# Hybrid decoder block: the order of the first projections, the engines of their weight splits, and transposes whose results nobody reads

## The chip, the cores and the metric

The kernel runs on one core of a Trainium2 chip. The metric is device time in microseconds (us): the median of three runs of the unprofiled kernel. Beside it there is one profiled execution, from which all rows below come. Lower is better.

## The reference

One layer over 1024 tokens, to which 16 learned meta tokens are prepended (1040 in all), with 1024 features:

```
u    = rms_norm(h, norm_mix)                      # h: 1040 x 1024
proj = u @ w_in                                   # attention A, attention B, xc, yc, gates
xc   = causal_depthwise_conv(xc)                  # width 4
o_c  = rg_lru(xc) * gelu(yc)                      # recurrence over tokens, 512 channels
o_a  = sliding_window_attention(.., rel_bias)     # 8 heads, relative bias table
o_f  = forgetting_attention(..)                   # 8 heads
h    = h + (sum_g sigmoid(gate_g) * (o_g @ w_branch_g)) @ w_out
h    = h + swiglu(rms_norm(h, norm_ffn))
out  = rms_norm(h, norm_final)[16:]
```

Only the start of this concerns the change: the first norm, the projections of xc and yc for the first two of four groups of 128 channels, and the relative bias table (32 buckets x 8 heads, gathered by a matrix product with a one-hot table of 383 distances).

## The kernel before

All matrix products are made in three terms: each operand is split into a high part (rounded to TensorE's short fp32 form, a copy on ScalarE) and a low part (the difference, on VectorE, or on GpSimd where `lo_on_pool` is given), and `mm3` (L143) adds high x high, high x low and low x high, for 8 slices of 128 features: 24 matmuls for each group of 128 channels and each chunk of tokens.

The tokens come in nine tiles: tile 0 holds the 16 meta tokens, tiles 1 to 8 hold 128 tokens each. `load_x` fetches a tile (512 KB, four buffers), `normed` squares and sums it on ScalarE (L297), takes the root there (L298), the reciprocal on VectorE (L299), and multiplies by that and the gain row `gbc` on VectorE in two halves (L301). `to_feature_major` (L198) then makes eight 128x128 transposes on TensorE (L204), four to a PSUM bank, and splits each bank into `uh` and `ul` (L118 on ScalarE, L119 on VectorE).

`proj_chunk` projects one chunk of tokens for one group of channels. The chunks are written out by hand:

```
FULL = ((0, 0, 272, 0), (0, 272, 256, 272), (1, 0, 512, 528))   # block, offset, tokens, position
REAL = ((0, NM, 512, 0), (1, 0, 512, 512))
```

`FULL` serves xc (meta tokens too), `REAL` serves yc. `FULL[0]` needs tiles 0, 1 and 2; `FULL[1]` needs tiles 3 and 4; `REAL[0]` needs tiles 1 to 4; `FULL[2]` and `REAL[1]` need tiles 5 to 8.

Before the change the order in the program is: tiles 0, 1, 2; the bias table's product; the two weight groups `wx` of xc (high part L137 on ScalarE, low part L138 on GpSimd); tiles 3 and 4; `FULL[0]` and `FULL[1]` of xc for both groups; the weights `wy` of yc (low part on GpSimd too); tiles 5 and 6; `REAL[0]` of yc for group 0; tiles 7 and 8; the bias table's spread over 128 partitions by two transfers (`bb`, then `bss`); `REAL[0]` for group 1; then `FULL[2]` and `REAL[1]` for both groups. All of this lives in a pool `r0`, whose memory the next stage (the recurrence, with the third and fourth group's projections as its main stream) takes over tile by tile as it comes free.

All transfers are issued from SyncE's queue. A scheduler orders each engine's instructions by their place in the program and by its own estimate of when their inputs are ready, so that an engine's order is not always that of the text. `keep_in_program_order` pins an instruction to its place; `issue_after(x)` queues the instructions of a block that run on x's engine behind x.

Of the kernel before, what the change touches and what calls it, by code (L numbers as in the profile page):

```python
# [9 lines left out]
F32 = mybir.dt.float32  # L10
F32R = mybir.dt.float32r
AF = mybir.ActivationFunctionType
ALU = mybir.AluOpType
# [3 lines left out]
P = 128  # L17
D = 1024
KT = D // P
NM = 16  # L20
# [14 lines left out]
QA, KA, QF, KF, XC, YC, GT = 0, 4, 5, 9, 13, 17, 21  # L35
# [11 lines left out]
def f32(ap):  # L47
    return ap.bitcast(F32)
# [3 lines left out]
def hybrid_block(ctx, tc, h_in, w_in, w_v0, w_v1, w_bd, par, rows, gains, relt, onehot,  # L52
                 maskrow, cmask, w_br, w_out, w_fi, w_fo, out):
    nc = tc.nc
    act, dve, pool, pe = nc.scalar, nc.vector, nc.gpsimd, nc.tensor

    def dma(dst, src):
        nc.sync.dma_start(f32(dst) if dst.dtype == F32R else dst, f32(src) if src.dtype == F32R else src)
# [8 lines left out]
    wp = ctx.enter_context(tc.tile_pool(name="wstream", bufs=2, side="left"))  # L67
# [11 lines left out]
    def nm(s):  # L79
        uid[0] += 1  # L80
        return f"{s}_{uid[0]}"

    def bank(tag, bufs, label):
        return pp.tile([P, 512], F32, tag=tag, bufs=bufs, name=nm(tag + label))
# [4 lines left out]
    o_bank = lambda label="": bank("ob", 1, label)  # L89
# [6 lines left out]
    ident = cp.tile([P, P], F32, name="ident")  # L96
    make_identity(nc, ident)
    cmt = cp.tile([P, P], F32, name="cmt")
    part = cp.tile([P, 40], F32, name="part")
    rowt = cp.tile([P, 16], F32, name="rowt")  # L100
    nsink = cp.tile([P, 8], F32, name="nsink")
# [13 lines left out]
    def split(hi, lo, src, scale=None, pin=False):  # L115

        if scale is None:
            act.activation(hi, src, AF.Copy)  # L118
            i = dve.tensor_tensor(lo, src, f32(hi), ALU.subtract)  # L119
            if pin:  # L120
                tc.keep_in_program_order(i)
        else:
            act.activation(hi, src, AF.Copy, scale=scale)
            dve.scalar_tensor_tensor(lo, src, scale, f32(hi), ALU.mult, ALU.subtract)

    def load_w(src, n, pl=None, tag="w", bufs=None, lo_on_pool=False):
        pl = pl or wp
        kw = {} if bufs is None else dict(bufs=bufs)
        if n == D:
            raw = wp.tile([P, n], F32, tag="wr", name=nm("wr"))  # L130
        else:
            raw = pl.tile([P, n], F32, tag=tag + "r", name=nm(tag + "r"), **kw)
        dma(raw, src)
        hi = pl.tile([P, n], F32R, tag=tag + "h", name=nm(tag + "h"), **kw)
        lo = pl.tile([P, n], F32R, tag=tag + "l", name=nm(tag + "l"), **kw)
        if lo_on_pool:
            act.activation(hi, raw, AF.Copy)  # L137
            pool.tensor_tensor(lo, raw, f32(hi), ALU.subtract)  # L138
        else:
            split(hi, lo, raw)  # L140
        return hi, lo
# [12 lines left out]
    def run(gen):  # L154
        for _ in gen:
            pass
# [41 lines left out]
    def to_feature_major(xg, n, uh, ul, off):  # L198

        for half in range(2):  # L200
            pt = tr_bank()
            for i in range(4):
                k = 4 * half + i
                pe.transpose(pt[:, i * P:i * P + n], xg[:n, k * P:(k + 1) * P], ident[:n, :n])  # L204
            src = pt.rearrange("p (i q) -> p i q", i=4)[:, :, :n]
            ks = slice(4 * half, 4 * half + 4)
            split(uh[:, ks, off:off + n], ul[:, ks, off:off + n], src)

    def u_tile(c, a):
        if c:  # L210
# [4 lines left out]
    uh = [u_tile(c, "h") for c in range(2)]  # L215
    ul = [u_tile(c, "l") for c in range(2)]
    FULL = ((0, 0, 272, 0), (0, 272, 256, 272), (1, 0, 512, 528))
    REAL = ((0, NM, 512, 0), (1, 0, 512, 512))

    def proj_chunk(j, w, chunk, sink):  # L220
        c, off, n, t0 = chunk
        ps = mm_bank(f"_w{j}")
        yield from mm3(ps[:, :n], [(w[0][:, k * P:(k + 1) * P], w[1][:, k * P:(k + 1) * P],
                                    uh[c][:, k, off:off + n], ul[c][:, k, off:off + n]) for k in range(KT)])
        sink(ps, n, t0)
# [36 lines left out]
    def x_sinks(pl, m):  # L262
        xr = pl.tile([P, 3 + T], F32, tag="xr", bufs=4, name=nm("xr"))
        y = pl.tile([P, S], F32, tag="y", bufs=4, name=nm("y"))
        pool.memset(xr[:, 0:3], 0.0)
        lru_in[m] = (xr, y)

        def xsink(ps, n, t0):
            act.activation(xr[:, 3 + t0:3 + t0 + n], ps[:, :n], AF.Copy)

        def ysink(ps, n, t0):
            act.activation(y[:, t0:t0 + n], ps[:, :n], AF.Copy)
        return xsink, ysink

    ra = ctx1.enter_context(tc.tile_pool(name="ra", bufs=1, side="right", reuse_waits="tile"))
    pad(ra, 128)
    with tc.tile_pool(name="r0", bufs=1, side="right", reuse_waits="tile") as r0:
        gbc = r0.tile([P, D], F32, name="gbc")

        def rows_of(t):  # L280
            return (NM, 0) if t == 0 else (P, NM + (t - 1) * P)

        def load_x(t):
            n, t0 = rows_of(t)
            xt = r0.tile([P, D], F32, tag="xt", bufs=4, name=nm("xt"))
            dma(xt[:n], h_in[t0:t0 + n])
            return xt

        def norm_in(t, xt):
            to_feature_major(*normed(t, xt))  # L290

        def normed(t, xt):
            n, t0 = rows_of(t)
            c, off = (0, t0) if t0 < W0 else (1, t0 - W0)
            xg = r0.tile([P, D], F32, tag="xg", bufs=3, name=nm("xg"))
            q = cp.tile([P, 1], F32, tag="sq", bufs=4, name=nm("sq"))
            act.activation(xg[:n], xt[:n], AF.Square, accum_out=q[:n])  # L297
            act.activation(q[:n], q[:n], AF.Sqrt, bias=epst[:n], scale=1.0 / D)  # L298
            dve.reciprocal(q[:n], q[:n])  # L299
            for x, y, z in zip(*(halves(v[:n]) for v in (xg, xt, gbc))):  # L300
                dve.scalar_tensor_tensor(x, y, q[:n], z, ALU.mult, ALU.mult)  # L301
            return xg, n, uh[c], ul[c], off

        xts = [load_x(t) for t in range(2)]
        dma(gbc, gains[0:1].partition_broadcast(P))
        xts.append(load_x(2))
        n0, n1 = normed(0, xts[0]), normed(1, xts[1])
        to_feature_major(*n1)
        n2 = normed(2, xts[2])
        to_feature_major(*n0)  # L310
        to_feature_major(*n2)

        dma(cmt, cmask)
        rt = r0.tile([32, 8], F32, name="rt")
        oh = r0.tile([32, 383], F32, name="oh")
        mr = r0.tile([8, 383], F32, name="mr")
        dma(rt, relt)
        dma(oh, onehot)
        dma(mr, maskrow.partition_broadcast(8))
        pb = sc_bank()  # L320
        pe.matmul(pb[:8, :383], rt, oh, start=True, stop=True)
        dve.tensor_tensor(mr, pb[:8, :383], mr, ALU.add)
        sinks = [x_sinks(ra, m) for m in range(2)]
        wx = [load_w(w_in[XC + m], D, r0, f"x{m}", lo_on_pool=True) for m in range(2)]
        xs34 = [load_x(t) for t in (3, 4)]
        n34 = [normed(t, xs34[t - 3]) for t in (3, 4)]
        for m in range(2):
            run(proj_chunk(XC + m, wx[m], FULL[0], sinks[m][0]))
            if m == 0:
                to_feature_major(*n34[0])  # L330
                to_feature_major(*n34[1])
        for m in range(2):
            run(proj_chunk(XC + m, wx[m], FULL[1], sinks[m][0]))
        xs56 = [load_x(t) for t in (5, 6)]
        wy = [load_w(w_in[YC + m], D, lo_on_pool=True) for m in range(2)]
        for t in range(5, 7):
            norm_in(t, xs56[t - 5])
        run(proj_chunk(YC, wy[0], REAL[0], sinks[0][1]))
        for t in range(7, 9):
            norm_in(t, load_x(t))  # L340
        dma(part, par)
        dma(rowt, rows.partition_broadcast(P))
        dve.tensor_scalar(nsink, rowt[:, 0:8], -1.0, None, ALU.mult)
        dma(bts, mr)
        pad(r0, 32)
        bb = r0.tile([P, 8, 383], F32, name="bb")
        dma(bb, bts.partition_broadcast(P))
        dma(bss, bb)
        run(proj_chunk(YC + 1, wy[1], REAL[0], sinks[1][1]))
        for m in range(2):  # L350
            run(proj_chunk(XC + m, wx[m], FULL[2], sinks[m][0]))
        for m in range(2):
            run(proj_chunk(YC + m, wy[m], REAL[1], sinks[m][1]))
# [477 lines left out]
    with tc.tile_pool(name="r4", bufs=1, side="right", reuse_waits="tile") as r4:  # L831
        woh = r4.tile([P, KT, D], F32R, name="woh")
        wol = r4.tile([P, KT, D], F32R, name="wol")
        with tc.tile_pool(name="r4a", bufs=1, side="right", reuse_waits="tile") as r4a:
# [8 lines left out]
            for m in range(8):  # L843
                f, raw = ahead
# [13 lines left out]
        with tc.tile_pool(name="r4b", bufs=1, side="right", reuse_waits="tile") as r4b:  # L858
            for c in range(2):
                u2[c] = [pair_tile(mp if c else bp) for k in range(KT // 2)]  # L860
                for tt in range(4 * c, 4 * c + 4):
# [4 lines left out]
                    for half in range(2):  # L866
                        n = slice(512 * half, 512 * half + 512)
# [8 lines left out]
                    for half in range(2):  # L876
                        pt = tr_bank()
                        for i in range(4):
                            k = 4 * half + i
                            pe.transpose(pt[:, i * P:(i + 1) * P], xg[:, k * P:(k + 1) * P], ident)  # L880
                        for i in range(4):
                            k = 4 * half + i
# [339 lines left out]
```

## Time and profile before

| | us |
|---|---|
| median of 3 runs | 1662.91 (1661.93 to 1663.35) |
| the profiled execution's own time | 1662.29 |
| its span, first to last instruction | 1660.5 |

TensorE is busy for 98% of the span, VectorE for 60%, ScalarE for 46%, GpSimd for 26%. "Idle before" in a row is the time in which the engine did nothing before that instruction, with what ended it. The recorded granted clock of TensorE is 1.00 in every stretch up to 1037 us, also where matmuls follow each other at twice their later distance; the distances of starts are therefore what is read for the clock at the start.

### The profile page before, as it was taken

The numbers are of one execution on the slowest core, as the hardware profiler recorded it, in microseconds if no ns is written. First come the engines' busy times: TensorE is split into PE (matmuls) and PEld (weight loads), VectorE is DVE, ScalarE is ACT, GpSimd is POOL, SyncE is SP. The second block draws the span as 40 slices with busy tenths as digits, with TensorE's granted clock in tenths as the row PEclk, the third lists the DMA queues.
The fourth block names the chain that finished last, engine by engine and source line by source line (L and its number), as shares of the span: only waits on it lengthen the run. The fifth ranks groups of instructions, "written<-read, shape, count | busy, mean of one in ns | idle before, by whom it ended". The sixth has DMA issues, their size and how long they took to land.

```text
span 1660.5 us, 22597 instructions
## 1 busy us (share of the span) xinstructions
PE 1630.2 (98%) x8159; PEld 1375.1 (83%) x8159; DVE 999.4 (60%) x1799; ACT 760.7 (46%) x1397; POOL 433.1 (26%) x341
## 2 busy tenths in 40 slices
PE   7999999999999999999999999899999999999998
PEld 6898978888888888888887888688888888888886
DVE  6565556555566666641348437977666676567544
ACT  6456466555555555542336434333333333345342
POOL 2111001001122221110225001776666566300000
PEclk9999999999999999999999999899999999999999
DMA  7132352223324142339737221464444443598642
GB/s 255 63 108 93 122 153 79 88 89 121 108 76 129 59 122 79 107 114 320 244 127 235 102 77 70 158 222 169 165 147 146 146 161 131 197 356 278 195 128 101
DMA packets 110879, 242.47 MB, mean 146 GB/s; under 512 B 11944, under 2 KB 23544, under 8 KB 110512
## 3 DMA queue, kind: packets, MB, share of 16 engines
q1 hardware_dynamic: 110768, 241.04, 42.7%
q8 instruction: 64, 1.05, 0.3%
q14 instruction: 47, 0.39, 0.1%
HBM read 163.45 MB, written 72.21 MB: 142 GB/s over the span
## 4 chain that ended last, share of the span: by engine, by line
PE 87%; DVE 4%; issue 4%; ACT 2%; POOL 1%; DMA 1%; SPq 0%; DVEq 0%; POOLq 0%; ACTq 0%
PE mm_w L150 26%; PE mm_s L150 13%; PE tr_s L150 7%; PE mm_br L150 6%; PE mm_wo L150 5%; PE mm_x L1086 4%; PE tr_y L1086 4%; PE sc_y L1086 4%; PE ob L547 3%; PE sc_s L150 3%; PE tr L558 3%; PE mm_v L150 2%; PE ob_x L1086 1%; PE mm_g L150 1%; PE mm_u L150 1%
## 5 line engine op out<-in xcount | busy, mean ns | idle before, releaser
L150 PE MATMUL mm_w<-uh,wh 128*128 128x512 f32 (+2 forms) x744 | 292.6, 393 | 0.0
L150 PE MATMUL mm_w<-uh,wl 128*128 128x512 f32 (+2 forms) x744 | 280.5, 377 | 0.0
L150 PE MATMUL mm_w<-ul,wh 128*128 128x512 f32 (+2 forms) x744 | 279.9, 376 | 0.0
L150 PEld LDWEIGHTS mm_w<-uh,wl 128*128 128x128 f32 x744 | 140.0, 188 | 25.7
L150 PEld LDWEIGHTS mm_w<-uh,wh 128*128 128x128 f32 x744 | 140.4, 189 | 12.7
L150 PEld LDWEIGHTS mm_w<-ul,wh 128*128 128x128 f32 x744 | 140.7, 189 | 11.7
L119 DVE TENSOR_TENSOR ab<-raw,ab 128x1024 fp32r<-128x1024 f32 x77 | 93.0, 1224 | 71.6 <-ACT ab L118 69.6
L118 ACT ACTIVATE ab<-raw 128x1024 fp32r<-128x1024 f32 x77 | 80.9, 1059 | 94.7 <-PE ob_x L1086 23.4
L150 PE MATMUL mm_s<-pt,ar 128*128 128x512 f32 x480 | 117.4, 394 | 3.7 <-ACT c L952 3.7
L118 ACT ACTIVATE wh<-wr 128x1024 fp32r<-128x1024 f32 (+1 forms) x85 | 72.7, 856 | 103.2 <-PE mm_w L150 50.6
L150 PE MATMUL mm_br<-o,wh 128*128 128x512 f32 x384 | 118.3, 389 | 0.0
L119 DVE TENSOR_TENSOR pl<-tr,ph 128x384 fp32r<-128x384 f32 (+2 forms) x160 | 87.4, 555 | 47.0 <-ACT ph L118 43.1
L150 PEld LDWEIGHTS mm_s<-pt,ar 128*128 128x128 f32 x480 | 91.5, 191 | 23.6 <-ACT c L952 4.5
L118 ACT ACTIVATE ph<-tr 128x384 fp32r<-128x384 f32 (+2 forms) x160 | 76.8, 485 | 53.6 <-PE tr L558 51.5
L119 DVE TENSOR_TENSOR wl<-wr,wh 128x1024 fp32r<-128x1024 f32 x45 | 55.6, 1235 | 72.2 <-ACT wh L118 71.9
L648 POOL TENSOR_SCALAR s<-s,sm 128x144 f32<-128x144 f32 (+3 forms) x64 | 48.6, 761 | 172.1 <-DVE sm L647 144.2
L150 PEld LDWEIGHTS mm_br<-o,wh 128*128 128x128 f32 x384 | 72.1, 188 | 14.9
L558 PE MATMUL tr<-ident,s 128*128 128x128 f32 x480 | 79.6, 274 | 1.2 <-POOL s L596 0.6
L150 PE MATMUL mm_wo<-woh,hl 128*128 128x512 f32 x256 | 79.1, 390 | 0.0
L150 PE MATMUL mm_br<-o,wl 128*128 128x512 f32 x192 | 75.3, 392 | 1.5 <-DVE wl L119 1.4
L558 PEld LDWEIGHTS tr<-ident,s 128*128 128x128 f32 x480 | 59.1, 140 | 18.3 <-DVE pl L119 3.4
L1086 PE MATMUL mm_x<-ab 128*128 128x512 f32 x297 | 72.7, 389 | 0.0
(252 smaller groups left out, 3687.9 us busy)
## 6 DMA issues: line engine op xcount, KB each, us to landing
wr<-w_in_dram SPq DMA_DIRECT2D x45, 512.0 KB, 3.7
wr<-w_fi_dram SPq DMA_DIRECT2D x44, 512.0 KB, 3.8
raw<-asp SPq DMA_DIRECT2D x77, 256.0 KB, 3.2
asp<-a SPq DMA_DIRECT2D x66, 256.0 KB, 2.5
gz<-z SPq DMA_DIRECT2D x48, 256.0 KB, 2.1
o<-osp SPq DMA_DIRECT2D x24, 512.0 KB, 6.1
sg<-gz SPq DMA_DIRECT2D x48, 256.0 KB, 3.2
fo<-w_fo_dram SPq DMA_DIRECT2D x22, 512.0 KB, 5.1
```

The costliest lines, as they stand in the source:

```text
L118: act.activation(hi, src, AF.Copy)
L119: i = dve.tensor_tensor(lo, src, f32(hi), ALU.subtract)
L150: pe.matmul(ps, a, b, start=first and i == 0, stop=i == n - 1, skip_group_check=not first)
L547: pe.matmul(ob[:, q0:q0 + b - a], vt[:, c], x[:, a:b], start=count == 0, stop=count == n_mm - 1, skip_group_check=True)
L558: pe.transpose(tb[:, col:col + P], src, ident)
L648: pool.tensor_scalar(s[:, :nk], s[:, :nk], den, 1.0, ALU.mult, ALU.mult)
L1086: pe.matmul(banks[x], a[:, 0, q], b[:, 1], start=first and j == 0 and c == 0, stop=j == NJ - 1 and c % 3 == 2, skip_group_check=True)
```

## The change

Tiles 3 and 4 are loaded and normed first and `FULL[1]` of xc is projected first; then tiles 1, 2 and 0, the second half of the old `REAL[0]` of yc, `FULL[0]` of xc, tiles 5 to 8, and the first half of the old `REAL[0]`. Each of yc's first chunks of 512 tokens becomes two of 256. The low parts of `wx` and `wy` go from GpSimd to VectorE. ScalarE's high parts of `wx` are queued behind the last split of tile 3 and tile 4, its norm work for tiles 1, 2 and 0 behind that of tile 4. `busy` issues transposes into a PSUM bank that is not read: 16 of the identity matrix at the start, 8 behind each of tiles 3 and 4. The bias table's product, its mask and `nsink` are pinned behind these projections and ahead of `FULL[2]`; the table's transfers follow.

```diff
-        xts = [load_x(t) for t in range(2)]
+        def busy(x, n, k):
+            for i in range(k):
+                pe.transpose(spare[:, :n], x[:n, i * P:(i + 1) * P], ident[:n, :n])
+
+        spare = o_bank("_spare")
+        for _ in range(16):
+            busy(ident, P, 1)
+
+        xts = {3: load_x(3)}
         dma(gbc, gains[0:1].partition_broadcast(P))
-        xts.append(load_x(2))
-        n0, n1 = normed(0, xts[0]), normed(1, xts[1])
-        to_feature_major(*n1)
-        n2 = normed(2, xts[2])
-        to_feature_major(*n0)
-        to_feature_major(*n2)
+        xts[4] = load_x(4)
+        raws = []
+        for m in range(2):
+            raws.append(wp.tile([P, D], F32, tag="wr", name=nm("wr")))
+            dma(raws[m], w_in[XC + m])
+        sinks = [x_sinks(ra, m) for m in range(2)]
+        wx = []
+        ns = [normed(t, xts[t]) for t in (3, 4)]
+        for n, raw in zip(ns, raws):
+            seen = to_feature_major(*n)[0]
+            with tc.issue_after(seen):
+                hi, lo = (r0.tile([P, D], F32R, name=nm("wx")) for _ in range(2))
+                split(hi, lo, raw)
+                wx.append((hi, lo))
+            busy(n[0], P, 8)
+        xts = {t: load_x(t) for t in (1, 2, 0)}
+        wy = [load_w(w_in[YC + m], D) for m in range(2)]
+        for m in range(2):
+            run(proj_chunk(XC + m, wx[m], FULL[1], sinks[m][0]))
+        with tc.issue_after(seen):
+            for t in (1, 2, 0):
+                norm_in(t, xts[t])
+        for m in range(2):
+            run(proj_chunk(YC + m, wy[m], (0, 272, 256, 256), sinks[m][1]))
+        for m in range(2):
+            run(proj_chunk(XC + m, wx[m], FULL[0], sinks[m][0]))
+        for t in range(5, 9):
+            norm_in(t, load_x(t))
+        for m in range(2):
+            run(proj_chunk(YC + m, wy[m], (0, NM, 256, 0), sinks[m][1]))
+        dma(part, par)
+        dma(rowt, rows.partition_broadcast(P))
...
-        pe.matmul(pb[:8, :383], rt, oh, start=True, stop=True)
-        dve.tensor_tensor(mr, pb[:8, :383], mr, ALU.add)
...
+        tc.keep_in_program_order(pe.matmul(pb[:8, :383], rt, oh, start=True, stop=True))
+        tc.keep_in_program_order(dve.tensor_tensor(mr, pb[:8, :383], mr, ALU.add))
+        tc.keep_in_program_order(dve.tensor_scalar(nsink, rowt[:, 0:8], -1.0, None, ALU.mult))
         dma(bts, mr)
         pad(r0, 32)
         bb = r0.tile([P, 8, 383], F32, name="bb")
         dma(bb, bts.partition_broadcast(P))
         dma(bss, bb)
-        run(proj_chunk(YC + 1, wy[1], REAL[0], sinks[1][1]))
```

`split` and `to_feature_major` now return their last instructions, for `issue_after`. In the lines left out the old order of the weights, the tiles and the projections goes.

## Rows read from the trace of the kernel before

**Rows 1.** The page's busy time by engine.
```profile
PE 1630.2 (98%) x8159; PEld 1375.1 (83%) x8159; DVE 999.4 (60%) x1799; ACT 760.7 (46%) x1397; POOL 433.1 (26%) x341
```

**Rows 2.** Windows: stretch, length, busy us by engine, clock, DMA share, GB/s.
```profile
70.00:166.00 96.00, 94.46 (x571) 86.93 (x570) 59.67 (x118) 56.88 (x75) 19.34 (x8) 1.00 0.29 97
166.00:250.00 84.00, 81.59 (x449) 71.19 (x447) 49.88 (x73) 43.90 (x72) 6.27 (x6) 1.00 0.41 137
```

**Rows 3.** TensorE's timeline from its first instruction: start, us, line, tiles, shape.
```profile
9.07 1.94 PE L204 MATMUL tr<-ident,xg 128*128 128x128 f32 x8 [9.07 <-DVE xg L301]
10.94 1.44 PE L321 MATMUL sc<-oh,rt 32*8 32x383 f32 x2
12.31 3.25 PE L204 MATMUL tr<-ident,xg 16*128 16x16 f32 x16
15.39 0.59 PE L150 MATMUL mm_w<-uh,x0h 128*128 128x272 f32 x1
...
19.00 0.43 PE L150 MATMUL mm_w<-ul,x0h 128*128 128x272 f32 x1
19.23 0.43 PE L150 MATMUL mm_w<-uh,x0l 128*128 128x272 f32 x1
...
19.77 0.29 PE L150 MATMUL mm_w<-uh,x0l 128*128 128x272 f32 x1
19.89 0.28 PE L150 MATMUL mm_w<-uh,x0h 128*128 128x272 f32 x1
...
28.73 0.28 PE L150 MATMUL mm_w<-uh,x1l 128*128 128x256 f32 x1
28.85 0.28 PE L150 MATMUL mm_w<-uh,x1h 128*128 128x256 f32 x1
...
31.01 1.03 PE L204 MATMUL tr<-ident,xg 128*128 128x128 f32 x8
31.80 0.48 PE L150 MATMUL mm_w<-uh,wh 128*128 128x512 f32 x1
...
33.72 0.66 PE L204 MATMUL tr<-ident,xg 128*128 128x128 f32 x4 [0.54 <-DVE ul L119]
...
48.19 0.39 PE L150 MATMUL mm_w<-uh,x0l 128*128 128x512 f32 x1
48.42 0.39 PE L150 MATMUL mm_w<-uh,x0h 128*128 128x512 f32 x1
...
68.14 0.29 PE L150 MATMUL mm_w<-uh,wh 128*128 128x272 f32 x1
```

**Rows 4.** ScalarE's timeline of the start.
```profile
8.63 1.06 ACT L297 ACTIVATE xg<-xt 128x1024 f32<-128x1024 f32 x1 [2.42 <-DMA xt<-h_in_dram]
...
10.19 0.60 ACT L118 ACTIVATE uh<-tr 128x512 fp32r<-128x512 f32 x1
...
11.54 1.05 ACT L137 ACTIVATE x0h<-wr 128x1024 fp32r<-128x1024 f32 x1
```

**Rows 5.** VectorE's timeline, up to 60 us.
```profile
6.86 2.73 DVE L301 SCALAR_TENSOR_TENSOR xg<-xt,sq,gbc 16x512 f32<-16x512 f32 x4 [0.45 <-DMA gbc<-gains_dram]
...
10.34 0.75 DVE L301 SCALAR_TENSOR_TENSOR xg<-xt,sq,gbc 128x512 f32<-128x512 f32 x1
11.01 0.68 DVE L119 TENSOR_TENSOR ul<-tr,uh 128x512 fp32r<-128x512 f32 x1
...
27.27 4.21 DVE L301 SCALAR_TENSOR_TENSOR xg<-xt,sq,gbc 128x512 f32<-128x512 f32 x2
...
59.04 1.23 DVE L119 TENSOR_TENSOR bdl<-wr,bdh 128x1024 fp32r<-128x1024 f32 x1 [3.74 <-ACT bdh L118]
```

**Rows 6.** GpSimd's timeline: the low parts of yc's weights.
```profile
25.70 5.22 POOL L138 TENSOR_TENSOR wl<-wr,wh 128x1024 fp32r<-128x1024 f32 x2 [8.33 <-ACT wh L137]
```

**Rows 7.** SyncE's timeline: the issue of the bias table's last transfer.
```profile
38.78 0.33 SPq L58 DMA_DIRECT2D bss<-bb x1
```

**Rows 8.** The page's transfers: count, KB each, median us to landing.
```profile
wr<-w_in_dram SPq DMA_DIRECT2D x45, 512.0 KB, 3.7
```

More of the change, by code (lines that the diff above doesn't have):

```diff
@@ L117, in split @@
         if scale is None:
-            act.activation(hi, src, AF.Copy)
+            a = act.activation(hi, src, AF.Copy)
             i = dve.tensor_tensor(lo, src, f32(hi), ALU.subtract)
@@ L122, in split @@
         else:
-            act.activation(hi, src, AF.Copy, scale=scale)
-            dve.scalar_tensor_tensor(lo, src, scale, f32(hi), ALU.mult, ALU.subtract)
+            a = act.activation(hi, src, AF.Copy, scale=scale)
+            i = dve.scalar_tensor_tensor(lo, src, scale, f32(hi), ALU.mult, ALU.subtract)
+        return a.ins, i.ins
     def load_w(src, n, pl=None, tag="w", bufs=None, lo_on_pool=False):
@@ L206, in to_feature_major @@
             ks = slice(4 * half, 4 * half + 4)
-            split(uh[:, ks, off:off + n], ul[:, ks, off:off + n], src)
+            last = split(uh[:, ks, off:off + n], ul[:, ks, off:off + n], src)
+        return last
     def u_tile(c, a):
@@ L320, in hybrid_block @@
         pb = sc_bank()
-        pe.matmul(pb[:8, :383], rt, oh, start=True, stop=True)
-        dve.tensor_tensor(mr, pb[:8, :383], mr, ALU.add)
[L323 to L343, printed above, removed]
+        tc.keep_in_program_order(pe.matmul(pb[:8, :383], rt, oh, start=True, stop=True))
+        tc.keep_in_program_order(dve.tensor_tensor(mr, pb[:8, :383], mr, ALU.add))
+        tc.keep_in_program_order(dve.tensor_scalar(nsink, rowt[:, 0:8], -1.0, None, ALU.mult))
         dma(bts, mr)
```

## The prediction

> **What bounds the kernel now.** Read the busy times first: TensorE works for 98% of the span [rows 1], so a change at the start can give back only what TensorE loses there, and every microsecond won there moves all that follows. The change ends where the next stage's first matmul (272 tokens of the third channel group) starts, at 68.14 us [rows 3]; I call that point the end of the stage, and forecast how far it moves.
>
> How much is lost before it? TensorE's timeline gives the prices. At the upper level of the clock (2.4 GHz) starts are 0.12 us apart for 272 and for 256 tokens, and 0.227 us for 512 [rows 3]; eight transposes take 31.80 - 31.01 = 0.79 us, 0.10 each [rows 3]. The stage holds 6 chunks of 512 (144 x 0.227 = 32.7), two of 272 and two of 256 (96 x 0.12 = 11.5) and 72 transposes (7.1): 51.3 us. It ends at 68.1, so 16.8 us are lost. The same timeline says where: nothing before 9.07; then transposes, the table's product and waits up to 15.39; then matmuls 0.23 apart up to about 19.5, twice their later distance, which is the lower level of 1.2 GHz [rows 3]; later one wait of 0.54 [rows 3]. In a change that fetches other tiles first the question is how early the first dense run of projections can begin, and at which level.
>
> **The first norms.** ScalarE waited 2.42 us for the third tile, up to 8.63 [rows 4], and VectorE for the gain row up to 6.86 [rows 5]: the start is set by landings. The new order has tile 3, the gain row, tile 4: the 64 KB of the meta tokens and one issue leave the front. I take 0.45 us off both: the gain row at 6.4, tile 4 at 8.2. One half of a norm's product takes 0.7 us [rows 5], so TensorE has its first useful transpose at about 7.2 in place of 9.07. That is not yet the gain, since projections need tile 4 too. From its landing to the product is 10.34 - 8.63 = 1.7 us [rows 4, 5], the first half 0.75: 10.65. Four transposes at the lower level (1.94 / 8 = 0.24 each [rows 3]) end at 11.6, ScalarE's split takes 0.60 [rows 4], VectorE's 0.68 [rows 5]: 12.9 for the chain by itself.
>
> **What queues beside that chain.** VectorE: from 9.9 it has the two halves for tile 4 (1.5), both low parts of tile 3 (1.4), the low part of the first weight group (1.23, the price of the same shape at 59.04 [rows 5]) and the first low part of tile 4 (0.7): 14.7 if all stand ahead, 12.9 if none does. TensorE: the eight idle transposes behind tile 3 end at about 11.1 (two banks from 7.2, then 1.94), those of tile 4 behind them at 13.0 at the earliest, and the eight idle ones of tile 4 take another 1.94 if they stand ahead of the projection, as they do in the program: 14.9. ScalarE has, from 8.2, the norm (1.6), the splits (2.4) and one weight group (1.05 [rows 4]): 13.3. Dense projections thus begin between 12.9 and 15; I take 14.6, near the two longer queues. The row of before is 15.39.
>
> **The clock.** In before, 24 transposes and the table's product from 9.07 to 15.5 left the matmuls behind them at 0.23; the distance fell to 0.12 some 4.1 us after the first of them [rows 3]. The product loads few rows of the array and eight transposes are of 16 tokens, so this is strong and not conclusive evidence that transposes don't lift the clock. I take it that they don't: 16 + 8 + 8 idle ones then buy nothing, the first 16 cost nothing (TensorE waits for tile 3 anyway), and the first 4.1 us of projections run at the lower level as before, for an extra 4.1 x (1 - 0.12 / 0.23) = 2.0 us.
>
> **What the stage then holds, from 14.6.** yc's first halves as four chunks of 256: 96 x 0.12 = 11.5 in place of 48 x 0.227 = 10.9, so splitting them costs 0.6. xc's `FULL[1]` and `FULL[0]`: 11.5. The 512 chunks left: 96 x 0.227 = 21.8. Seven tiles' transposes: 5.5; tiles 0 to 2 were in the waiting time before 15.39 and now stand between projections. The table's product, 1.44 at the lower level beside idle time [rows 3], comes into the dense stretch: bounds 0 and 1.44, I take half, 0.7. Sum 51.0, and 2.0 for the clock: 14.6 + 53.0 = 67.6.
>
> **Stalls on the way.** VectorE, from 9.9, needs 1.5 + 2.7 + 2.5 us for tiles 3 and 4 and `wx` (16.6), then for tiles 1, 2, 0 and `wy` 3.1 + 3.1 + 1.8 + 2.5 (27.1). TensorE, from 14.6, is through `FULL[1]` at 22.4, through the transposes of 1, 2, 0 at 24.8, and through the first two of yc's half chunks (5.8) at 30.6. The work fits in sum; in sequence, `wy`'s first low part can be late: its raw buffer is free after the first `wx` low part (about 14), the load takes 3.7 [rows 8], ScalarE 1.05, so VectorE can have it done at 20.1, or at 25.9 if the three norms go first, 1.1 after TensorE wants it. Bounds 0 and 1.1; I take 0.6. A relief on the other side: GpSimd's low parts (5.22 for two) ran beside two half products that took 4.21 in place of 1.4 [rows 5, 6], and the 0.54 wait [rows 3] came after them; both are gone, and the count from 14.6 already has no such wait. End of the stage: 68.2, against 68.14.
>
> **The table's transfers.** The product now runs at about 68.2 - 21.8 - 0.7 = 45.7; before, it ran at 10.94 and `bss` was issued at 38.78 [rows 3, 7]. Two small steps and the same 7 us for `bb` put `bss` at about 56 and its landing at 61. What lies behind it in memory is written by the next stage only later, and TensorE needs the next weights at 68; I cost this at 0, covered by the two rows of 512 chunks that follow the product. The pinned VectorE steps wait for that product with no norm left behind them.
>
> **The sum.** 1662.29 (the profiled execution, 0.62 below the median of the runs shown) + 0.1 = 1662.4 us. That is no change: about 0.2% (3.3 us) is what a measurement of this kernel can tell from none.
>
> **Rivals.** *Idle transposes hold the clock up.* For it: nothing in before runs so many of full size so early. Against it: the 24 that were followed by slow matmuls [rows 3]. It would take off the 2.0 and shorten the idle and useful transposes ahead of the projections, so that these begin at 13.4: 68.2 - 2.0 - 1.2 = 65.0, 3.2 less, 1659.2. The Trainium skill ("TensorE: Matmul & The Clock Gate", Part 4: PE-mode transpose) says that the full clock does not engage for transposes, as they don't count as activity of the engine in the same way: it speaks against what these idle transposes could be for. By that rule the time is my forecast, by its opposite this rival's; rows 3 agree with it as far as they go.
>
> *VectorE becomes the bound, and the kernel slower.* Four low parts of 1.23 (4.9 us) leave GpSimd, which was idle 74% of the time [rows 1], for VectorE, in its fullest 20 us. If its order puts them ahead of splits that TensorE waits for, or the norms ahead of `wy`, up to 4.9 us come onto TensorE, 4.3 beyond the 0.6 counted: 1666.7. It decides from the point at which VectorE is through `wy`'s low parts later than 28.5 us, or the first projection starts after 17.
>
> *The table's transfers hold the next weights back.* If these stand behind `bss` on SyncE's queue, they are issued at 56.5, land at 60 to 64 and are split 2 to 4 us later; above 66 the next stage starts late, by up to 3 us: 1665.3.
>
> *Later queues come out in another order.* The scheduler's estimates shift for all that follows; TensorE is idle 1.5 us between 70 and 166 and 2.4 between 166 and 250 [rows 2], which could vanish or double: 4 us to either side at most, as a spread on each case.
>
> **How the numbers follow.** Forecast (lower clock, no bound from VectorE) 0.60, by itself 1660 to 1665; clock held 0.20; VectorE 0.13; table 0.07. With the spread, more than 0.2% faster holds 0.10 of the first and 0.10 of the second: 0.20. Slower holds 0.06 of the first, 0.11 of the third, 0.03 of the last: 0.20. Within 0.2%: 0.60. The range reaches from a little below the held clock (1658.5) to VectorE's case (1667.0); some 0.1 lies outside on either side.
>
> **What would show it.** Useful transposes from about 7.2; the first projection near 14.6, its matmuls 0.21 to 0.23 apart for about 4 us; 256 token chunks at 0.12; the product behind them at 45 to 46; the next stage's first matmul at 68. Matmuls at 0.12 from the first one on would show the first rival; waits of TensorE for `ul`, `wl` or `wx` above 2 us in sum the second; one at 68 for the third group's weights the third.

## The result and the profile after

The changed kernel takes 1666.05 us (median of 9 runs, 1663.45 to 1668.03), beside 1662.02 for the kernel before: a ratio of 1.0023, 95% interval 1.0014 to 1.0032. It is slower by 0.23%. The forecast was 1662.4, no change; the time came out near the upper end of the range. The profiled execution has a span of 1664.4 us (its own time 1666.20), 3.9 more than before. The lines of the new kernel are shifted: `mm3` is L151, the transposes L205, `busy` L309, a norm's product L303, the table's product L359, and the text behind the stage is 17 lines lower.

The page's busy time by engine [rows 1]: the shares stay, POOL gives 7 us away and VectorE takes 3.

```profile
PE 1635.2 (98%) x8239; PEld 1382.2 (83%) x8239; DVE 1002.7 (60%) x1803; ACT 760.8 (46%) x1399; POOL 425.8 (26%) x337
```

The windows of the two stretches behind the stage, after [rows 2]. TensorE is idle for 2.5 and 4.0 us of them where it was 1.5 and 2.4, and the granted clock of the first is no longer 1.00:

```profile
70.00:166.00 96.00, 93.51 (x553) 85.67 (x551) 63.52 (x125) 56.73 (x75) 20.05 (x9) 0.98 0.29 97
166.00:250.00 84.00, 80.00 (x437) 69.86 (x437) 48.51 (x58) 40.83 (x60) 5.27 (x4) 1.00 0.40 136
```

TensorE's timeline of the start, after [rows 3]:

```profile
1.45 3.67 PE L309 MATMUL ob_spare<-ident 128*128 128x128 f32 x16 [1.45 <-POOL ident masks.py:199]
7.40 1.94 PE L205 MATMUL tr<-ident,xg 128*128 128x128 f32 x8 [2.28 <-DVE xg L303]
9.13 1.85 PE L309 MATMUL ob_spare<-ident,xg 128*128 128x128 f32 x9
11.46 0.66 PE L205 MATMUL tr<-ident,xg 128*128 128x128 f32 x4 [0.47 <-DVE ul L119]
...
12.55 0.82 PE L309 MATMUL ob_spare<-ident,xg 128*128 128x128 f32 x6
13.12 0.36 PE L151 MATMUL mm_w<-uh,wx 128*128 128x256 f32 x1
13.79 0.38 PE L151 MATMUL mm_w<-ul,wx 128*128 128x256 f32 x1 [0.30 <-DVE ul L119]
14.01 0.40 PE L151 MATMUL mm_w<-uh,wx 128*128 128x256 f32 x2
...
22.85 0.66 PE L205 MATMUL tr<-ident,xg 128*128 128x128 f32 x4 [0.35 <-DVE ul L119]
...
44.34 0.81 PE L359 MATMUL sc<-oh,rt 32*8 32x383 f32 x2
45.08 0.50 PE L151 MATMUL mm_w<-uh,wx 128*128 128x512 f32 x1
...
67.26 0.29 PE L151 MATMUL mm_w<-uh,wh 128*128 128x272 f32 x1
```

Eight transposes still take 1.94 us from 7.40, the price of the lower level; four from 11.46 take 0.66, the price of the upper one. The clock rises inside the idle transposes: those behind tile 3 start 0.21 apart up to 10.41 and 0.11 apart from 10.60. The trace's own record of the granted clock begins with this change, at 10.57 (in the kernel before at 19.58, where its matmuls close up to 0.12); ahead of its first entry the views print 1.00, so that the 1.00 of the first stretch says nothing about the start. The projections start at 13.12 with their matmuls 0.12 apart; none of them runs at double distance. Two waits for a low part interrupt them, of 0.55 behind 13.12 and of 0.51 ahead of 22.85, from start to start and less the usual 0.12 (the idle times in the rows, 0.30 and 0.35, count from a modelled end). The stage ends at 67.26, which is 0.88 earlier than before [rows 3]. VectorE's timeline behind the first tile shows what stands ahead of the second tile's splits [rows 5]; on ScalarE [rows 4] the second norm starts at 7.68, and GpSimd has no low part left [rows 6]:

```profile
9.39 1.42 DVE L303 SCALAR_TENSOR_TENSOR xg<-xt,sq,gbc 128x512 f32<-128x512 f32 x2
10.72 1.28 DVE L119 TENSOR_TENSOR ul<-tr,uh 128x512 fp32r<-128x512 f32 x2
11.92 1.21 DVE L119 TENSOR_TENSOR wx<-wr,wx 128x1024 fp32r<-128x1024 f32 x1
13.05 1.28 DVE L119 TENSOR_TENSOR ul<-tr,uh 128x512 fp32r<-128x512 f32 x2
```

SyncE's timeline has the issue of the table's last transfer [rows 7]:

```profile
53.36 0.32 SPq L58 DMA_DIRECT2D bss<-bb  x1
```

So the stage was won and the kernel lost. To find where, I set the start of every instruction against that of its partner in the trace before. TensorE leads by 0.88 us at 67 and by 0.57 at 100 to 114; it trails by 1.98 at 120, by 3.53 at 250, and by 3.92 at the end. From 250 to 1050 the difference falls by 0.3, and near 1070, at a wait for ScalarE, it rises by 0.65. Two places decide, and the first is the seventh tile of the value projection. TensorE's timeline of it, after:

```profile
114.13 0.31 PE L151 MATMUL mm_v<-vh,ul 128*128 128x328 f32 x1
116.86 0.61 PE L151 MATMUL mm_v<-vh,uh 128*128 128x328 f32 x1 [2.42 <-DVE zall L485]
...
119.46 0.47 PE L151 MATMUL mm_v<-vh,uh 128*128 128x328 f32 x1
119.73 0.35 PE L151 MATMUL mm_v<-vl,uh 128*128 128x328 f32 x1
```

and the same of the kernel before:

```profile
114.71 0.31 PE L150 MATMUL mm_v<-vh,ul 128*128 128x328 f32 x1
116.23 0.39 PE L150 MATMUL mm_v<-vh,uh 128*128 128x328 f32 x1 [1.21 <-DVE zall L468]
116.45 0.31 PE L150 MATMUL mm_v<-vl,uh 128*128 128x328 f32 x1
116.60 0.31 PE L150 MATMUL mm_v<-vh,ul 128*128 128x328 f32 x1
```

TensorE needs `zall`'s bank free, and VectorE reads it at the end of a long chain. VectorE's step in after:

```profile
116.56 0.15 DVE L485 TENSOR_TENSOR zall<-mm_v,rowt 128x8 f32<-128x8 f32 x1
```

and in before:

```profile
115.92 0.16 DVE L468 TENSOR_TENSOR zall<-mm_v,rowt 128x8 f32<-128x8 f32 x1
```

TensorE arrived 0.58 earlier and VectorE's step came 0.63 later, so the wait doubled from 1.21 to 2.42. And behind the longer wait the matmuls are 0.27 apart in place of 0.15 until 119.73: the clock has fallen, by the trace's record at 116.38, inside the wait. The ten distances from 116.86 to 119.73 take 2.87 us, and would take 0.22 + 9 x 0.15 = 1.57 at the distances of before: 1.3 us on top of 1.2.

Why was VectorE late, in a stretch that the change doesn't touch? ScalarE's timeline at the end of the stage, after:

```profile
62.02 0.60 ACT L274 ACTIVATE y<-mm_w 128x512 f32<-128x512 f32 x1 [3.89 <-PE mm_w L151]
62.64 1.28 ACT L163 ACT_TABLE_LOAD   x1
63.93 0.20 ACT L163 ACTIVATE ls<-ls 128x4 f32<-128x4 f32 x1
```

and before:

```profile
59.03 1.28 ACT L162 ACT_TABLE_LOAD   x1
60.32 0.20 ACT L162 ACTIVATE ls<-ls 128x4 f32<-128x4 f32 x1
...
63.69 0.58 ACT L272 ACTIVATE y<-mm_w 128x512 f32<-128x512 f32 x1
```

The scheduler has changed the order: the copy of yc's projection (`y`) now stands ahead of the exponential of the decay's log-sigmoid (`ls`). The copy waits 3.89 us for TensorE, and the table load and the exponential queue behind it; they come 3.6 us later than before. VectorE has `ls` next in its own queue and stands still, in after:

```profile
64.17 0.17 DVE L164 TENSOR_SCALAR ls<-ls 128x4 f32<-128x4 f32 x1 [4.78 <-ACT ls L163]
64.25 1.29 DVE L386 SCALAR_TENSOR_TENSOR x<-xr,part,x 128x1040 f32<-128x1040 f32 x1
```

The convolution's taps (`x`) behind it start at 64.25, in before 3.6 us sooner:

```profile
60.64 1.29 DVE L369 SCALAR_TENSOR_TENSOR x<-xr,part,x 128x1040 f32<-128x1040 f32 x1
```

That is the first stage of the recurrence, whose scan VectorE has to finish ahead of `zall`.

The second place is at 245 us, the first scores of the window attention. TensorE loses 1.5 us there, since the bias row (`nb`) lands late; VectorE's row of it:

```profile
247.14 0.37 DVE L603 CUSTOM_DVE_ANT_0 s<-sc,nb,nsink 128x144 f32<-128x144 f32 x1 [3.74 <-DMA nb<-bss]
```

In before the same step waits 1.73 us, and TensorE not at all:

```profile
243.19 0.37 DVE L586 CUSTOM_DVE_ANT_0 s<-sc,nb,nsink 128x144 f32<-128x144 f32 x1 [1.73 <-DMA nb<-bss]
```

### The profile page after: what moved, and what is told of

The parts are those of the page before. It is cut to its first block, busy times and chain, and to the rows that moved or that the text cites. A ratio compares the mean times of both kernels' runs of the same rounds, so it can differ in the third digit from the quotient of the medians.

```text
span 1664.4 us, 22764 instructions
## 1 busy us (share of the span) xinstructions
PE 1635.2 (98%) x8239; PEld 1382.2 (83%) x8239; DVE 1002.7 (60%) x1803; ACT 760.8 (46%) x1399; POOL 425.8 (26%) x337
## 4 chain that ended last, share of the span: by engine, by line
PE 83%; DVE 6%; issue 5%; ACT 2%; DMA 2%; POOL 1%; SPq 0%; DVEq 0%; POOLq 0%; ACTq 0%
PE mm_w L151 23%; PE mm_s L151 13%; PE tr_s L151 7%; PE mm_br L151 6%; PE mm_wo L151 5%; PE mm_x L1103 4%; PE tr_y L1103 4%; PE sc_y L1103 4%; PE ob L564 3%; PE sc_s L151 3%; PE tr L575 3%; PE mm_v L151 2%; PE ob_x L1103 1%; PE mm_g L151 1%; PE mm_u L151 1%
## 5 line engine op out<-in xcount | busy, mean ns | idle before, releaser
L151 PE MATMUL mm_w<-uh,wh 128*128 128x512 f32 (+2 forms) x760 | 295.6, 389 | 0.0
L151 PE MATMUL mm_w<-uh,wl 128*128 128x512 f32 (+2 forms) x760 | 283.3, 373 | 0.0
L151 PE MATMUL mm_w<-ul,wh 128*128 128x512 f32 (+2 forms) x760 | 282.9, 372 | 0.0
L151 PEld LDWEIGHTS mm_w<-uh,wl 128*128 128x128 f32 x760 | 143.0, 188 | 25.1
L151 PEld LDWEIGHTS mm_w<-uh,wh 128*128 128x128 f32 x760 | 143.5, 189 | 12.3
L151 PEld LDWEIGHTS mm_w<-ul,wh 128*128 128x128 f32 x760 | 143.8, 189 | 11.3
L118 ACT ACTIVATE ab<-raw 128x1024 fp32r<-128x1024 f32 x77 | 80.8, 1059 | 91.9 <-DMA raw<-w_fo_dram 22.4
L151 PE MATMUL mm_s<-pt,ar 128*128 128x512 f32 x480 | 117.9, 395 | 4.7 <-ACT c L969 4.7
L151 PE MATMUL mm_br<-o,wh 128*128 128x512 f32 x384 | 118.3, 389 | 0.0
L151 PEld LDWEIGHTS mm_s<-pt,ar 128*128 128x128 f32 x480 | 91.7, 191 | 24.4 <-ACT c L969 5.2
L151 PEld LDWEIGHTS mm_br<-o,wh 128*128 128x128 f32 x384 | 72.1, 188 | 14.9
L151 PE MATMUL mm_wo<-woh,hl 128*128 128x512 f32 x256 | 79.1, 389 | 0.0
L151 PE MATMUL mm_br<-o,wl 128*128 128x512 f32 x192 | 75.2, 392 | 1.5 <-DVE wl L119 1.4
```

What stands on the lines that cost most here:

```text
L118: a = act.activation(hi, src, AF.Copy)
L151: pe.matmul(ps, a, b, start=first and i == 0, stop=i == n - 1, skip_group_check=not first)
```

## The experiments

All were timed beside runs of the kernel before on the same chip. "Shift" is TensorE's lag behind the profile of before. The times of the kernel before itself, over all these runs, have a median of 1662.6.

**The changed kernel again.** No edit.

> The changed kernel once more, unaltered. My theory: the stage ends at 67.3 us, 0.9 earlier than before, but a later wait of TensorE in the value projections (2.4 us at 115, against 1.2 before) ends 0.6 later and lets its clock fall, so that 2.0 us are lost there; 1.5 more come near 245 us, where a bias tile lands late. If both are tied to the instruction order they stand in this profile too, within 0.3 us. Rival: the two are chance of one execution; then at least one is missing here, and the time is spread over 1663 to 1668 us.

1664.77 us (11 runs, 1663.16 to 1668.80) beside 1662.70: 1.0019 [1.0010, 1.0028]. The stage ends at 67.92, and the wait is there, but the clock doesn't fall behind it; TensorE's timeline there:

```profile
117.64 0.39 PE L151 MATMUL mm_v<-vh,uh 128*128 128x328 f32 x1 [2.54 <-DVE zall L485]
```

At 245 only 0.14 is lost, and this execution took 1663.2 in all. So the longer wait came with the order of instructions both times; the fall of the clock and the loss at 245 come in some executions and not in others. The 20 runs of this kernel spread over 5.6 us, with 7 below 1665 and 13 above 1665.4.

**Without the idle transposes.**

```diff
-        spare = o_bank("_spare")
-        for _ in range(16):
-            busy(ident, P, 1)
...
-            busy(n[0], P, 8)
```

> The changed kernel without the 16 + 8 + 8 idle transposes. If they hold the clock up: first matmuls 0.21 us apart for about 4 us in place of 0.12, stage end 67.3 + 1.5 to 2.0 = 69 us, and the time 0 to 2 us above the changed kernel's (0 if the later stall on ScalarE's and VectorE's chain absorbs it). If they do nothing for the clock: same spacing as with them, 67.3, and no change. If they cost: up to 1 us less.

1665.00 (1664.01 to 1667.45) beside 1662.70: 1.0020 [1.0011, 1.0028]. TensorE's timeline:

```profile
13.28 0.58 PE L151 MATMUL mm_w<-uh,wx 128*128 128x256 f32 x1
...
16.73 0.41 PE L151 MATMUL mm_w<-ul,wx 128*128 128x256 f32 x1
16.95 0.59 PE L151 MATMUL mm_w<-uh,wx 128*128 128x256 f32 x2
17.37 0.29 PE L151 MATMUL mm_w<-ul,wx 128*128 128x256 f32 x1
```

Now the matmuls are 0.21 apart (16.73 to 16.95, and two more up to 17.37) until 17.4, 4.1 us from the first, as I had forecast for the change itself. The stage ends at 68.38, some 0.5 to 1.1 later than in the two profiles with them (but `a_fill` below has them too, and its stage ended at 69.06). The wait for `zall` doesn't absorb this: it is as long as with them (2.49 us), since VectorE's step comes later by as much as TensorE does. The median is 0.2 above the one of the changed kernel beside it (1664.77), and these two sets of 11 runs, spread over 3.4 and 5.6 us, can't tell a cost of 0.5 to 1.1 from none.

**The low parts of the weights on GpSimd again.**

```diff
-                split(hi, lo, raw)
+                act.activation(hi, raw, AF.Copy)
+                pool.tensor_tensor(lo, raw, f32(hi), ALU.subtract)
...
-        wy = [load_w(w_in[YC + m], D) for m in range(2)]
+        wy = [load_w(w_in[YC + m], D, lo_on_pool=True) for m in range(2)]
```

> The changed kernel with the low parts of both weight pairs on GpSimd again. My theory: VectorE was not the bound; the stage ends within 0.7 us of 67.3, the time within 1 of the changed kernel's. Rival (VectorE, which took over 4.9 us of work, holds TensorE back): stage end 65.5 or less and 1663 or less. A low part on GpSimd takes 2.4 us in place of 1.2, so the first projections may start up to 2 us later.

1665.88 (1664.69 to 1669.13) beside 1662.70: 1.0022 [1.0013, 1.0031]. The stage ends at 68.66, 1.4 later than in the changed kernel, where I had expected 0.7 at most; the wait for `zall` is 2.36 us, and the clock falls behind it. TensorE's stalls in the stage are not smaller than with the low parts on VectorE. VectorE, with four low parts more, isn't what makes the kernel slow.

**The decay's log-sigmoid early, first try.** Its exponential and its small VectorE steps leave the end of the stage and stand ahead of `FULL[2]`, behind the last tile's split; so nothing is left that the copy of yc could hold back.

```diff
-            norm_in(t, load_x(t))
+            seen8 = to_feature_major(*normed(t, load_x(t)))[0]
...
+        with tc.issue_after(seen8):
+            log_sigmoid(lsc[:, 1], part[:, P_LM:P_LM + 4], cp, [P, 4])
+        dve.tensor_scalar(lsc[:, 0], lsc[:, 1], -4.0, None, ALU.mult)
+        dve.tensor_scalar(lsc[:, 1], lsc[:, 1], 8.0, None, ALU.mult)
         for m in range(2):
             run(proj_chunk(XC + m, wx[m], FULL[2], sinks[m][0]))
...
-        log_sigmoid(lsc[:, 1], part[:, P_LM:P_LM + 4], r1, [P, 4])
-        dve.tensor_scalar(lsc[:, 0], lsc[:, 1], -4.0, None, ALU.mult)
-        dve.tensor_scalar(lsc[:, 1], lsc[:, 1], 8.0, None, ALU.mult)
```

> The changed kernel with the log-sigmoid of the recurrence's decay (one Exp and 20 small VectorE steps) computed ahead of the last 512 token projections. My theory: in the changed kernel this Exp stands behind yc's copy on ScalarE, which waits for TensorE until 62 us, and VectorE's convolution steps behind it are 3.6 us late; without that the chain that ends the wait at 117 us ends about 0.6 to 1.5 us earlier, the wait falls to under 1.8 and the clock doesn't fall: 2 to 3 us below the changed kernel, 1663 to 1664. Rival (the order of ScalarE there doesn't matter): 1666, the same wait.

1700.62 beside 1662.70: 1.0233 [1.0219, 1.0247], far off what either theory expected. Up to 230 us it did what the first one said: shift -0.85, the wait short (1.18), no fall of the clock. At 245 it lost 1.0, and its shift at 735 is -0.61. Then comes one new wait, the longest in the view of waits:

```profile
PE mm_br L151 <- ACT wh L118: 25.6, 1, 25.6
```

Its four small tiles, 64 bytes per partition in all, lay in a pool that lives to the end (`cp`), and moved the place of everything that is put behind it on that side of the memory. That they did this by other tiles' waits for reused memory is an inference; what is shown is that the next run, whose only difference is the pool, doesn't have this wait.

**The same, with the tiles in a pool of the first stage** (`r0` in place of `cp`).

> As a_exp (the log-sigmoid ahead of the last 512 token projections), but its four small tiles lie in the stage's own pool behind the bias table, so that no later tile moves in memory. a_exp was 0.85 us ahead of the kernel before up to 740 us, with a wait of 1.2 at 114 and no fall of the clock, and lost 36 us at the branch weights. My theory: 1661 to 1662.5, 3 to 4 below the changed kernel, wait of 1.2 to 1.4 at 114. Rival (the loss lies in the log-sigmoid's place itself): near 1698 again.

1663.52 (1661.44 to 1665.94) beside 1662.33: 1.0007 [0.9999, 1.0016]. The stage ends at 67.21, and TensorE's timeline shows the wait of before, with the lead kept:

```profile
115.38 0.39 PE L151 MATMUL mm_v<-vh,uh 128*128 128x328 f32 x1 [1.25 <-DVE zall L486]
```

Shift -0.88 at 100 and still -0.75 at 230 us. Some 2.3 us of the loss (1665.9 is the median of the 20 runs of the changed kernel; resampling the runs leaves 0.9 to 3.4) were the order on ScalarE and what the doubled wait did. In this profile 1.0 is lost at 245, where `nb` is late again (VectorE waits 3.17 for it), and 0.3 later.

**The kernel before with the early log-sigmoid.** The same edit in the order of before.

> The kernel before with the same early log-sigmoid. If its late place costs only where yc's copy stands ahead of the Exp (as in the changed kernel): within 1 us of the kernel before, wait at 114 unchanged at 1.2. If it is a cost in any order: 1 to 3 us less than before.

1662.85 (1662.36 to 1663.35) beside 1662.33: 1.0005 [0.9996, 1.0014]. The wait for `zall` is 1.25, as it was. The edit is worth 2.3 us in the new order and nothing in the old one: it isn't a gain of its own, it takes away what the change had brought. In the old order the exponential stands ahead of yc's copy anyway.

**The kernel before with idle transposes.** 16 at the start and 8 behind tile 1.

```diff
+        spare = o_bank("_spare")
+        for _ in range(16):
+            busy(ident, P, 1)
...
         to_feature_major(*n1)
+        busy(n1[0], P, 8)
```

> The kernel before with 24 idle transposes alone: 16 of the identity at the start and 8 behind tile 1's. If idle transposes lift the clock by themselves, the matmuls from 15.4 are 0.12 us apart from the first on, the stage's end is 1.5 to 2 us earlier (66.2 to 66.6 in place of 68.1), and the time 1 to 2 us lower if the wait at 114 doesn't take it back, unchanged if it does (wait 2.7 or more). If they don't: 0.23 apart up to about 19.5 as before, no change.

1662.93 (1661.68 to 1664.19) beside 1662.33: 1.0003 [0.9994, 1.0012]. TensorE's timeline:

```profile
10.61 1.92 PE L306 MATMUL ob_spare<-ident,xg 128*128 128x128 f32 x8
...
16.79 0.59 PE L150 MATMUL mm_w<-uh,x0h 128*128 128x272 f32 x1
...
18.32 0.29 PE L150 MATMUL mm_w<-ul,x0h 128*128 128x272 f32 x1
```

The eight push the first projection from 15.39 to 16.79; the upper level is there at 18.3, 1.5 us behind the first matmul in place of 4.2. The kernel before has done that in one execution without them (last experiment), so this says little of what the eight lift. The 16 at the start did lift the clock, with nothing to use it: their last distance is 0.17, and the trace's record has the upper level at 4.60 and the lower one again at 8.02, in the pause behind them; the 16 transposes from 8.87 then all ran 0.21 apart. Neither expectation of the stage came out: the matmuls are not 0.12 apart from the first on, nor slow up to 19.5, and the stage ends at 69.30, 1.2 later than before, with the later start and a wait of 1.3 for a low part in it.

**The changed kernel with 16 transposes in the wait for `zall`.**

```diff
+            if i == 1 and t == 6:
+                fb = o_bank("_fill")
+                for _ in range(16):
+                    tc.keep_in_program_order(pe.transpose(fb[:, :P], ident, ident))
             ps = mm_bank(f"_v{t}")
```

> The changed kernel with 16 transposes of the identity ahead of the seventh tile of the value projections, in the wait at 114 to 117 us. If the wait's idle time is what lets the clock fall in some executions: the fall doesn't come in the profile, the runs spread less (changed kernel: 1663.2 to 1668.8), median 0.5 to 1.5 us below the changed kernel's 1664.8 to 1666. If the fall has another cause: same median and spread; the 1.7 us of transposes lie in the wait and cost nothing either way.

1663.97 (1662.54 to 1665.55) beside 1662.33: 1.0012 [1.0003, 1.0021]. TensorE's timeline at the wait:

```profile
116.30 1.91 PE L481 MATMUL ob_fill<-ident 128*128 128x128 f32 x16
118.82 0.39 PE L151 MATMUL mm_v<-vh,uh 128*128 128x328 f32 x1 [0.61 <-DVE zall L489]
```

The chain of VectorE is as late as in the changed kernel, but TensorE is idle for 0.61 us only; no fall of the clock, and no run above 1665.55, where 11 of 20 of the changed kernel were. The median is 0.45 above the one with the early log-sigmoid, less than the runs can tell, so the medians don't say how the 2.3 us divide between the longer wait and the fall of the clock. This execution's stage ended late (69.06, with a wait of 1.9, start to start, for a low part at 22.6), so its single profile says nothing of the median.

**The bias row ahead of the value load.** The kernel with the early log-sigmoid, and in the window attention:

```diff
-                            if head % 4 == 0:
-                                vt = load_v(head // 4)
                             bt = at([P, T], F32, "nb", 2)[:, :256]
...
+                            if head % 4 == 0:
+                                vt = load_v(head // 4)
```

> The changed kernel with the decay's log-sigmoid early (as in the run before last of that kind) and, in the first attention stage, the bias transfer of a head (128 KB) placed ahead of the load of the value tile (512 KB) that stood in front of it. Theory (the loss near 245 us is the bias transfer issued behind the value load, 2 to 3 us late): TensorE's lead of 0.75 us over the kernel before, which held up to 230 us and was lost at 245, stays; the end of the trace is 0.7 us ahead of before's 1660.5, and the median is 1662.5, about 1.0 below the 1663.5 without this edit. Rival (the transfer's landing is set by the memory traffic, not by its place in the queue): the loss of about 1.0 at 245 remains, and the median stays at 1663.5.

1663.67 (1662.34 to 1665.55) beside 1662.74: 1.0008 [0.9999, 1.0016]. The rival's number came out, not its mechanism. The transfer is issued 2.3 us earlier, and the step that reads the row starts 2.2 earlier (243.86 without this edit), so its place in the queue does count. But the scheduler puts the scores ten matmuls earlier as well. VectorE still waits for the row:

```profile
241.67 0.37 DVE L604 CUSTOM_DVE_ANT_0 s<-sc,nb,nsink 128x144 f32<-128x144 f32 x1 [0.83 <-DMA nb<-bss]
```

and TensorE for VectorE, as before; 0.6 is lost there:

```profile
242.10 0.39 PE L602 MATMUL sc<-k,q 128*128 128x256 f32 x1 [0.67 <-DVE sm L604]
```

**The bias table's product behind `FULL[1]` as well** (its loads and the pinned matmul moved there, the rest left), on top of the edit just shown.

> The same, and the bias table's product moved out of the dense stretch to the place behind the first two projections of xc, where TensorE waits up to 0.5 us for a low part anyway. Theory (the product costs 0.9 us where it stood, and a lead passes the wait at 115 us unless the VectorE chain there ends later): end of the stage at 66.4 in place of 67.2, shift at 100 us about -1.7, and a median 0.8 below that of the kernel without this edit, 1661.7. Rival (the wait at 115 us is set by the VectorE chain, which doesn't come earlier): the stage ends 0.8 earlier, the wait grows by 0.8, and the median doesn't move.

1663.38 (1662.15 to 1666.17) beside 1662.74: 1.0007 [0.9998, 1.0016]. The product runs at 19.54, takes 0.74 there, and the wait of 0.3 that stood at 22.4 is one of 0.2 at 23.2; the stage ends at 66.99, 0.34 earlier than without this edit, where I had expected 0.8. The shift at 100 is -1.09, where I had expected -1.7, and passes the wait for `zall` (1.25 us), so that part of the theory held; at 245 it loses 1.2. The median was to be 1661.7; the two medians differ by 0.3 in that direction, less than these runs can tell.

**The kernel before with the bias row ahead.**

> The kernel before with only the bias transfer ahead of the value load. In its profile TensorE lost nothing at 245 us, so the theory that a loss there comes in some executions only gives 1662.0, at most 0.3 below the kernel before. Rival (the bias transfer is late in most executions of the kernel before too, and its profile caught a good one): 1661.5 or less.

1662.26 (1661.56 to 1662.82) beside 1662.74: 0.9998 [0.9989, 1.0007]: no change, and no wait at 245. But this profile shows something that I had not looked for. Up to the scores near 240 it holds the instructions of before in their order, and its stage ends at 66.73, not 68.14. TensorE's timeline:

```profile
15.24 0.59 PE L150 MATMUL mm_w<-uh,x0h 128*128 128x272 f32 x1
...
16.59 0.32 PE L150 MATMUL mm_w<-uh,x0h 128*128 128x272 f32 x1
16.74 0.29 PE L150 MATMUL mm_w<-ul,x0h 128*128 128x272 f32 x1
```

The upper level is there 1.5 us behind the first matmul. In the order of before the 4.1 us on which my sum rests are one of several outcomes: 4.2 and 4.5 in two profiles, 1.5 in this one.

## Why the prediction was wrong

*Front of the stage.* Right: the first useful transpose at 7.40 (forecast 7.2), tile 4's product at 9.39 (9.9).

*Start of the projections, 14.6.* Too late: the first matmul is at 13.12, the second, which wants a low part, at 13.79. VectorE's queue had the order that I gave as its longest (14.7), but began 0.5 earlier, and its pieces follow each other closer than their durations (10.72 - 9.39 = 1.33 for 1.42). The last idle transposes ran 0.11 apart, not 0.24: six in 0.82.

*"I take it that they don't."* Wrong. In the eight profiles with the new order and the idle transposes the distance of transposes falls to 0.11 between 10.2 and 13.2 us, ahead of the first matmul (in one of them already at 4.5, up again by 8.1, behind a pause, and down again by 11.7); without them, in the one profile taken, the rise is at 17.4. The 2.0 us that I charged for the lower level didn't arise. My evidence was one profile, in which the 24 transposes were 4.1 us from the rise; the runs show that this distance varies from execution to execution in the order of before. The Trainium skill ("TensorE: Matmul & The Clock Gate", Part 4: PE-mode transpose), by which the full clock doesn't engage for transposes, disagrees with these runs (starts 0.11 apart ahead of any matmul); the measurement decides.

*What the stage holds.* The 256-token chunks at 0.12 were right. The table's product cost 0.7 to 0.9 between dense matmuls (44.34 to 45.08, and a longer first matmul behind it), as taken. Forgotten: some 1.4 in all at the twelve groups of transposes, where the first matmul behind a group takes 0.20 in place of 0.12 and a group of four more than half of the 0.79 for eight. The stalls I had at 0.6 were 0.55 and 0.51, both for `ul`, none for `wl`. So the stage, from its first projection, lasted 54.1 in place of 53.6, although the 2.0 for the clock were not in it; it ended at 67.26, 0.9 before my 68.2. The first rival's condition came true and its start of 13.4 nearly so, but not its end of the stage (65.0), which leaves out the same terms, nor its 1659.2.

*VectorE as the bound.* It wasn't: it was through the low parts of `wy` at 22.2 (the sign was 28.5), the first projection was long before 17, and putting the low parts back on GpSimd changed nothing that the runs can tell. Its mechanism did show on a small scale: both stalls were for splits that stood behind a low part (11.92 and 20.97 on VectorE). *The table's transfers:* `bss` issued at 53.36 (forecast 56), nothing waited for it at the end of the stage; the cost of 0 was right. That the measured time lies near the second and third rivals' (1666.7 and 1665.3) is luck: neither cause came.

*The step that decided.* "Every microsecond won there moves all that follows" failed, and with it the term for later queues. The forecast was the stage's shift added to the old time, with the later queues as a spread of 4 us to either side around zero. Their order did change, in one place that could be named: yc's copy went ahead of the exponential. This delayed VectorE's chain up to `zall` (1.2 us of longer wait, 0.3 on the way to it), more than the stage had won, and in part of the executions let the clock fall (1.3). With 1.5 at 245 and 0.4 from there to the end that is 0.3 + 1.2 + 1.3 + 1.5 + 0.4 - 0.9 = 3.8 of the 3.9 in this execution. The direction of this term I had left open, though the row to look at stood in the profile: TensorE waits for the end of a VectorE chain (1.21 at 116.23), so whatever delays that chain costs TensorE as much.

All thirteen profiles show this term. VectorE's step at `zall` starts 47.8 to 47.9 us behind the end of the stage in the eight in which the exponential isn't held back by yc's copy, whether the stage ended at 66.73 or at 69.30, and the wait is 1.18 to 1.25 there. In the five in which it is, the step starts 49.3 to 49.5 behind the end of the stage: 1.5 later, each time. So a lead of the stage is not lost at this wait by itself; the chain follows the stage, and the order of ScalarE adds 1.5 to it.

*What stays open.* With the order on ScalarE mended the kernel is at 1663.55 in 33 runs of three variants, 1.0 above the 1662.6 of before, although TensorE led by 0.6 to 1.0 up to 230 us in all three profiles. It is lost at 245 (0.6 to 1.2) and near 1070 (0.2 to 0.8). In the profiles in the order of before, the loss at 245 was 0, 0, 0.6 and 0.9. It goes with the time from the issue of the bias row to the step that reads it: 3.8 to 4.3 us in the four profiles that lost 0.15 or less, and 4.65 to 5.8 in the other nine, of both orders. Why the row takes longer in some executions, and whether the new order makes that more frequent, these runs don't settle. No version was found that is measurably faster than the kernel before.

## What to carry to other kernels

A lead won on the bounding engine has to pass its first wait for another engine's chain; look for that wait in the trace of before, and ask what the chain hangs on and whether the change moves it too. When an edit shifts the scheduler's estimates, compare each engine's order far behind the edit: one small step behind a copy that waits can cost more than the stage had won. Where a clock's rise enters the sum, take it from several executions, since one profile shows one outcome.

## What the runs showed of the hardware

- Transposes of 128x128 in fp32 lifted TensorE's clock to its upper level (2.4 GHz), with nothing else on the engine: starts 0.21 apart, then 0.11, without a matmul ahead or between, in eight of eight profiles of the new order that have the idle ones. They didn't do it each time: in `b_idle` the 16 from 8.87 to 12.1 us stayed at 0.21.
- In or right behind a wait of 2.4 to 2.5 us the clock fell to the lower level (1.2 GHz) in two of four profiles. At the waits of 1.2 in this place it never fell, in eight profiles. The window from 114 to 122 us of the changed kernel's first profile, with a granted clock of 0.79:

```profile
114.00:122.00 8.00, 5.58 (x28) 5.34 (x28) 8.00 (x13) 1.98 (x4) 0.00 (x0) 0.79 0.53 213
```

and of the same kernel's second one, with 1.00:

```profile
114.00:122.00 8.00, 5.46 (x37) 5.22 (x36) 8.00 (x11) 2.74 (x5) 0.00 (x0) 1.00 0.45 180
```

- 64 bytes per partition in a long-lived pool made this kernel 37 us slower (1700.62 beside 1663.52), with one wait of 25.6 us and smaller losses behind it; how they did it is not shown.
